# Half of an attention stage's transposes moved from TensorE to VectorE blocks and a DRAM round trip

## The chip, the cores and the metric

The kernel runs on one core of one Trainium2 chip, in one launch. The metric is the device time of that core in microseconds. A core has four engines that matter here: TensorE (PE in the profile, with PEld for its weight loads), VectorE (DVE), ScalarE (ACT) and GpSimd (POOL). Most transfers are issued from SyncE's queue (SP), some from POOL's. All engines run at the same time, and each takes its own instructions strictly in order.

## The reference

The reference is one layer of a diffusion backbone in float32, with 1024 latent tokens, 256 context tokens and 1024 channels: a gated feed-forward block (2816 wide), a mixer, a second feed-forward block and a final norm. The mixer holds a short gated convolution branch and an attention branch, merged by gates and one output projection. Only the attention is touched by the change:

```python
def gqa_attend(q, k, v):
    s = jnp.einsum('btkgd,blkd->bkgtl', q, k, preferred_element_type=jnp.float32) * (HEAD_DIM ** -0.5)
    p = jax.nn.softmax(s, axis=-1).astype(v.dtype)
    return jnp.einsum('bkgtl,blkd->btkgd', p, v)
```

There are 8 query heads of 128 channels that share 2 key and value heads. The 1024 latent queries look at 256 context keys and 1024 latent keys in one softmax.

## The kernel before

Every large product is made of three TensorE passes over a rounded high part and a remainder (`mm3`): high x high, high x low, low x high. So each operand is split by two instructions: ACT rounds it to the high part, and DVE (or POOL) subtracts that to get the low part (`split`).

The kernel goes through the first feed-forward block, the projections into the mixer, attention with the convolution branch mixed in, the merge and output projection, the second feed-forward block and the final norm. Large tiles (4 KB a partition) come from one ring of 38 buffers, `atile`; smaller ones from `ttile`, weights from `wpool`, and TensorE's results from 8 banks of PSUM in three groups (`ps_s` five, `ps_t` two, `ps_o` one).

Attention is cut into 16 units (`class Unit`), one for each query head and each half of the queries (512 queries, `C0` or `C1`). A unit does the following:

- `begin` splits its queries into parts.
- `scores(qt)`, four times, for 128 queries each: products with the 256 context keys and twice 512 latent keys, DVE maxima over them, and ACT exponentials that are written to `pc` (context keys) and to one `pl` tile for each `qt` (latent keys), with the sums of their rows.
- `turn(kt)`, ten times, for 128 keys each (`kt` 0 and 1 are context keys): the exponentials lie with queries on the partitions, but the product with the values needs keys there. So TensorE transposes four 128 x 128 blocks, one for each `qt`, into one PSUM bank of `ps_t`, and `split` makes the two parts `pts` from it.
- `values(kt)`: three 512-wide matmuls that add this block's share to the output.
- `inverse` takes the reciprocals of the sums and spreads them over the partitions by two small transfers on POOL's queue (`rinvd`, `rrow`); `output` copies the result from PSUM with ACT, and POOL multiplies it by these rows.

The generator `seconds` runs the turns and values of all units one after another, with values three turns behind the turns (`AHEAD`). The loop `for n_unit, u in enumerate(units[1:], 1)` puts the pieces together: while the scores of unit n are made, ten steps of `seconds` run, those of unit n - 1, in groups of 3, 2, 3 and 2, each behind one block of scores. Between them stand pieces of `fillers`, the convolution products, about ten a unit, until they run out some four units before the end. From unit 13 on, `split_output` splits finished heads on POOL. Behind the loop come the turns and values of the last unit, and `merge`.

The kernel is written as one program in this order. A planner then fixes the order of each engine's instructions by a simulated time of each, close to the program's order, and allots buffers. The semaphores follow from what reads and writes which tile.

## Time and profile before

| | us |
|---|---|
| median of 3 runs | 2631.33 |
| lowest and highest run | 2630.29, 2632.03 |
| span of the profiled execution | 2631.1 |
| TensorE busy in it | 2609.9 |
| VectorE busy | 1997.4 |
| ScalarE busy | 1183.5 |
| GpSimd busy | 545.8 |
| attention stage, about | 1434 to 1822 |

The profile is that of one execution. Its span runs from the first to the last instruction. An engine's busy time is the time in which at least one of its instructions runs; consecutive matmuls overlap, so the distance from start to start tells more than a duration does. A group's row has the instruction, what it writes and from what, its shape, how many there are, their busy time in us and the mean of one in ns, and then how long the engine was idle before them and for whom it waited. In this kernel all instructions carry line 90, a helper, so groups are told apart by the names of their tiles.

### The profile page before, as it was taken

What the parts mean: (1) busy time and instruction counts of PE and PEld (TensorE: products, weight loads), DVE (VectorE), ACT (ScalarE), POOL (GpSimd) and SP (SyncE); (2) the same over time, 40 slices, a digit from 0 to 9 for tenths busy, and PEclk for the clock granted to TensorE, in tenths of its full rate; (3) what the DMA queues carried; (4) which work ended last, traced back from release to release, by engine and by line L of the source; (5) the groups of instructions that cost most, each with busy time, mean ns of one, the idle gap of its engine ahead of it and who ended that gap; (6) DMA issues with size and microseconds to landing.
All of it is one profiled execution on the core that took longest, in us unless ns stands there. A gap on an engine that the chain in (4) does not pass through costs nothing.

```text
span 2631.1 us, 35379 instructions
## 1 busy us (share of the span) xinstructions
PE 2609.9 (99%) x12665; PEld 2176.1 (83%) x12665; DVE 1997.4 (76%) x3360; ACT 1183.5 (45%) x2343; POOL 545.8 (21%) x425
## 2 busy tenths in 40 slices
PE   8999999999999999999999999999999999999998
PEld 5888899888888888888888888888888888888888
DVE  5888976877897879977788576676457886667996
ACT  6533454333454642333355566574237333334553
POOL 0133201221010034333022112132000442321100
PEclk9999999999999999999999999999999999999999
DMA  8665465345973365542522322113425653227831
GB/s 324 205 210 182 149 215 173 106 131 185 327 184 117 124 205 160 163 134 89 200 77 85 86 87 65 33 37 118 158 85 176 201 167 96 90 80 286 191 84 65
DMA packets 372905, 384.69 MB, mean 146 GB/s; under 512 B 19686, under 2 KB 256376, under 8 KB 372728
## 3 DMA queue, kind: packets, MB, share of 16 engines
q1 hardware_dynamic: 363288, 363.52, 42.1%
q0 software_dynamic: 9440, 18.91, 4.3%
q8 instruction: 99, 1.62, 0.2%
q14 instruction: 78, 0.64, 0.1%
HBM read 310.45 MB, written 71.86 MB: 145 GB/s over the span
## 4 chain that ended last, share of the span: by engine, by line
PE 94%; DVE 3%; DMA 1%; ACT 1%; issue 1%; SPq 0%; DVEq 0%; ACTq 0%
PE ps L90 81%; PE pt L90 8%; PE po L90 6%; DMA rawm<-in_w_mod_dram 1%; DVE xb L90 0%; DVE wl L90 0%; DVE macc L90 0%; DVE m L90 0%; DVE y L90 0%; DVE pts L90 0%; DMA xtok<-in_x_dram 0%; DVE x L90 0%; DVE r L90 0%; SPq L90 0%; DVE rs_t L90 0%
## 5 line engine op out<-in xcount | busy, mean ns | idle before, releaser
L90 PE MATMUL ps<-r,wl 128*128 128x512 f32 x5196 | 1198.3, 390 | 3.6 <-ACT r L90 1.3
L90 PEld LDWEIGHTS ps<-r,wl 128*128 128x128 f32 x5196 | 972.4, 188 | 207.7 <-ACT r L90 1.6
L90 ACT CAST wl<-sum 128x512 fp32r<-128x512 f32 x218 | 134.1, 622 | 294.4 <-PE ps L90 227.1
L90 ACT CAST wl<-raw 128x512 fp32r<-128x512 f32 x287 | 178.2, 622 | 193.1 <-PE ps L90 147.9
L90 DVE TENSOR_TENSOR wl<-raw,wl 128x512 fp32r<-128x512 f32 x287 | 210.2, 736 | 61.0 <-ACT wl L90 59.3
L90 DVE TENSOR_TENSOR wl<-sum,wl 128x512 fp32r<-128x512 f32 x218 | 196.9, 904 | 33.5 <-ACT wl L90 32.3
L90 POOL TENSOR_TENSOR sum<-raw 128x512 f32<-128x512 f32 x55 | 76.4, 1389 | 680.6 <-DMA raw<-in_ffn_w_in_dram 345.3
L90 DVE SCALAR_TENSOR_TENSOR macc<-rawm,silu_c,macc 128x512 f32<-128x512 f32 x178 | 145.4, 835 | 17.1 <-DMA rawm<-in_w_mod_dram 16.6
L90 DVE TENSOR_TENSOR u<-u,ps 128x512 f32<-128x512 f32 x186 | 126.5, 680 | 32.2 <-PE ps L90 32.1
L90 ACT CAST rh<-hid 128x512 fp32r<-128x512 f32 x132 | 82.2, 623 | 139.4 <-PE ps L90 112.3
L90 POOL TENSOR_TENSOR sum<-raw,sum 128x512 f32<-128x512 f32 x55 | 76.7, 1395 | 287.0 <-DVE wl L90 284.0
L90 DVE TENSOR_TENSOR pts<-pt,pts 128x512 fp32r<-128x512 f32 x160 | 107.3, 686 | 36.2 <-ACT pts L90 34.6
L90 DVE TENSOR_REDUCE m<-ps 128x1 f32<-128x256 f32 (+1 forms) x192 | 111.0, 597 | 29.4 <-PE ps L90 28.5
L90 ACT CAST pts<-pt 128x512 fp32r<-128x512 f32 x160 | 92.2, 597 | 85.5 <-PE pt L90 84.4
L90 PE MATMUL ps<-rh,wl 128*128 128x512 f32 x360 | 122.8, 390 | 0.0
L90 PE MATMUL ps<-wh,r 128*128 128x512 f32 x384 | 120.7, 392 | 0.0
L90 DVE TENSOR_TENSOR rl<-hid,rh 128x512 fp32r<-128x512 f32 x132 | 91.0, 693 | 29.9 <-ACT rh L90 19.4
L90 ACT CAST wh<-raw 128x512 fp32r<-128x512 f32 (+1 forms) x85 | 68.2, 803 | 95.5 <-PE ps L90 74.9
L90 PE MATMUL ps<-kl,qs 128*128 128x512 f32 x384 | 104.0, 394 | 0.1
L90 PE MATMUL ps<-rh,wh 128*128 128x512 f32 x300 | 102.8, 389 | 0.0
L90 PE MATMUL ps<-y,wc 128*128 128x512 f32 x384 | 95.3, 391 | 0.2 <-DVE g L90 0.2
L90 POOL TENSOR_TENSOR sum<-sum,raw 128x512 f32<-128x512 f32 x55 | 87.8, 1597 | 5.7 <-PE ps L90 3.9
(325 smaller groups left out, 5102.3 us busy)
## 6 DMA issues: line engine op xcount, KB each, us to landing
raw<-in_ffn_w_in_dram SPq DMA_DIRECT2D x131, 512.0 KB
raw<-in_ffn_w_out_dram SPq DMA_DIRECT2D x72, 512.0 KB
raw<-in_w_in_dram SPq DMA_DIRECT2D x64, 512.0 KB
rawm<-in_w_mod_dram SPq DMA_DIRECT2D x104, 256.0 KB
hid<-hd SPq DMA_DIRECT2D x40, 512.0 KB
ucd<-uc SPq DMA_DIRECT2D x33, 512.0 KB
rawm<-in_w_mod_dram SPq DMA_DIRECT2D x32, 512.0 KB
ws<-in_ffn_w_out_dram POOLq DMA_DIRECT2D x26, 512.0 KB, 6.4
```

The source lines that it names most:

```text
L90: inst = getattr(self.engine, name)(*args, **kw)
```

## The change

The queries of each unit are now treated in two halves. For its last 256 queries (`qt` 2 and 3), and for the context keys of all its queries, nothing changes but the tiles: TensorE transposes them. For the latent keys of the first 256 queries (`qt` 0 and 1):

- ACT writes the exponentials to a tile `pb` of 2048 columns, ordered by key block of 32, then `qt`, then key.
- `place` is a generator that is called between the steps. Two DVE instructions transpose `pb` in place, 1024 columns each, block by block of 32 x 32. Then four transfers on SP, one for each 32 partitions, write the blocks to a DRAM tile `turned` in pieces of 64 floats, and a fifth reads them back as `placed`, with the 128 keys of a key block on the partitions and 256 queries beside each other for each of eight key blocks.
- `turn(kt)` for latent keys transposes two blocks instead of four, and the split is done in two halves of 256 columns: ACT and POOL for `placed`, ACT and DVE for the PSUM bank.
- The first 256 queries of an output come in the order of blocks, so `output` copies them with a rearranged pattern, in an instruction of its own; the context keys' transposes write PSUM in the same order.

The buffers are divided: the ring `atile` has 28 instead of 38, and the space of the other ten is a second pool, `btile`. Ahead of the attention loop that pool is closed and opened again as five buffers of twice the size (`share("Q", Q_BUFS)`), for `pb`, `pl` and `placed`; behind it, as ten again. Many tiles of the other stages are assigned to the one or the other.

```diff
-A_BUFS = 38
+A_BUFS, B_BUFS, Q_BUFS = 28, 10, 5
...
         def begin(self):
             self.qs = [ttile("qs", dt=F32R) for _ in range(2)]
             split(q_of(self.hd, self.ch), *self.qs)
-            self.pc = atile("pc", (P, 4, CT))
-            self.pl = []
-            self.rsum = small("rsum", 4)
+            self.pc, self.pb, self.pl = atile("pc", (P, 4, CT)), btile("pb", (P, 2048)), btile("pl", (P, 2, SLOT))
+            self.done, self.rsum = 0, small("rsum", 4)
...
+            blocks = self.pb[:].rearrange("p (j b q c) -> p j q b c", j=2, q=2, c=32)
             for j in range(2):
                 ps = ps_s()
                 kh, kl = (t[:, g] for t in k_lat[j])
                 mm3(ps, [(qh, ql, kh, kl)])
                 dve.reduce_max(out=m3[:, j + 1 : j + 2], in_=ps, axis=AX.X)
-                parts.append((pl[:, j * 512 : (j + 1) * 512], ps))
+                if qt < 2:
+                    parts.append((blocks[:, j, qt], ps.rearrange("p (b c) -> p b c", c=32)))
+                else:
+                    parts.append((self.pl[:, qt - 2, j * 512 : (j + 1) * 512], ps))
...
+        def place(self):
+
+            for half in range(2):
+                part = self.pb[:, half * 1024 : (half + 1) * 1024]
+                dve.transpose(out=part, in_=part)
+                yield
+            turned = dram.tile([32, 32, 4, 64], F32, name=uniq("turned"))
+            for i in range(4):
+                sp.dma_start(
+                    out=turned[:, :, i].rearrange("b r f -> r b f"),
+                    in_=self.pb[i * 32 : (i + 1) * 32].rearrange("r (b f) -> r b f", b=32),
+                )
+            yield
+            self.placed = btile("placed", (P, KD, 256))
+            sp.dma_start(out=self.placed[:], in_=turned.rearrange("(k j) r i f -> (j r) k (i f)", j=4))
+
         def turn(self, kt):
 
-            pt = ps_t()
-            for qt in range(4):
-                src = self.pc[:, qt, kt * P : (kt + 1) * P] if kt < 2 else self.pl[qt][:, (kt - 2) * P : (kt - 1) * P]
-                transpose(pt[:, qt * P : (qt + 1) * P], src)
             pts = wpool.tile([P, 2, 512], F32R, tag="wh", name=uniq("pts"), bufs=W_BUFS)
-            split(pt, pts[:, 0], pts[:, 1])
+            if kt < 2:
+                pt = ps_t()
+                first = pt[:, :256].rearrange("p (i q c) -> p q i c", i=4, q=2)
+                for qt in range(4):
+                    out = first[:, qt] if qt < 2 else pt[:, qt * P : (qt + 1) * P]
+                    transpose(out, self.pc[:, qt, kt * P : (kt + 1) * P])
+                split(pt, pts[:, 0], pts[:, 1])
+            else:
+                pt = ps_t(256)
+                for qt in range(2):
+                    transpose(pt[:, qt * P : (qt + 1) * P], self.pl[:, qt, (kt - 2) * P : (kt - 1) * P])
+                split(self.placed[:, kt - 2], pts[:, 0, :256], pts[:, 1, :256], pool)
+                split(pt, pts[:, 0, 256:], pts[:, 1, 256:])
             return pts
...
         def output(self):
             of = q_of(self.hd, self.ch)
-            act.copy(out=of, in_=self.po)
+            v = lambda t, by: t[:, :256].rearrange(by, i=4, q=2)
+            act.copy(out=v(of, "p (q i c) -> p q i c"), in_=v(self.po, "p (i q c) -> p q i c"))
+            act.copy(out=of[:, 256:], in_=self.po[:, 256:])
             pool.tensor_mul(out=of, in0=of, in1=self.rows)
...
     for qt in range(4):
         u.scores(qt)
+        if qt == 2:
+            place = u.place()
+            run(place, 2)
+        if qt == 3:
+            run(place)
         if qt < 3:
             run(conv_out(C0, 2 + qt))
             conv_weights(4 + qt)
...
         for n in (3, 2, 3, 2):
-            u.scores(len(u.pl))
+            u.scores(u.done)
+            if u.done == 3:
+                place = u.place()
             for _ in range(n):
+                if u.done > 2:
+                    run(place, 1)
                 run(rest, 1)
-                if len(u.pl) < 4:
+                if u.done < 4:
                     run(fill, 1)
```

More of the change, by code (lines that the diff above doesn't have):

```diff
@@ L105, in tile_dit_layer, with share @@
     dram = ctx.enter_context(tc.tile_pool(name="dram", bufs=1, space=DRAM))
+    shared = {}
+    def share(tag, bufs):
+        if shared:
+            shared.pop("guard").__exit__(None, None, None)
+        guard = tc.tile_pool(name=uniq("share"), bufs=bufs, reuse_waits="tile")
+        shared.update(guard=guard, pool=guard.__enter__(), tag=tag)
     n_tiles = [0]
@@ L423, in tile_dit_layer, with __init__ @@
     class Context:
-        def __init__(self, name, dt=F32):
-            self.t = [atile(name, (P, 4, CT), dt) for _ in range(2)]
+        def __init__(self, name, dt=F32, get=btile):
+            self.t = [get(name, (P, 4, CT), dt) for _ in range(2)]
         def __call__(self, k, ch=CC):
@@ L475, in fetch_rows @@
     def fetch_rows(w, js):
-        ts = {j: atile("raw") for j in js}
+        ts = {j: btile("raw") for j in js}
         for j, t in ts.items():
@@ L735, in start_by_half @@
         def start_by_half(self):
-            uc = [atile("uc", (P, 2, 512)) for _ in range(2)]
+            uc = [btile("uc", (P, 2, 512)) for _ in range(2)]
             def second(j, t):
@@ L1402, in v_tile @@
         return v_hi[(kt - 2) // 4][:, (kt - 2) % 4], v_lo[(kt - 2) // 4][:, (kt - 2) % 4]
-    rope_t = [atile("rope", (P, KD, HD)) for _ in range(2)]
+    rope_t = [btile("rope", (P, KD, HD)) for _ in range(2)]
     for i in range(2):
         sp.dma_start(out=rope_t[i][:], in_=rope[i])
-    hg = atile("hg", (P, 2, HD))
+    hg = btile("hg", (P, 2, HD))
     pg = ps_t(2 * P)
@@ L1694, in merge @@
         yield
+    share("Q", Q_BUFS)
     units = [Unit(hd, ch) for hd in range(NQ) for ch in (C0, C1)]
@@ L1744, in tile_dit_layer @@
     split_output(NQ - 1, C1, late=True)
+    share("B", B_BUFS)
     for j in range(KD):
@@ L1752, in tile_dit_layer @@
     fast = Winograd(xs, None, modl, 6, column_pairs(ffn2_w_in[0], ffn_offsets), ahead=AH3)
+    fast.shared_forms = [(i, k) for i in (4, 7, 6) for k in range(4)][:B_BUFS]
     first = fast.norm0()
@@ L1861, in tile_dit_layer @@
     run(finals[2])
+    shared["guard"].__exit__(None, None, None)
 _INS = [
```

55 lines of the change are left out of this document (29 added, 26 removed).

## The prediction

> **What bounds the kernel now.** I read the page's totals and its chain of waits first.
>
> ```profile
> span 2631.1 us, 35379 instructions
> PE 2609.9 (99%) x12665; PEld 2176.1 (83%) x12665; DVE 1997.4 (76%) x3360; ACT 1183.5 (45%) x2343; POOL 545.8 (21%) x425
> PE 94%; DVE 3%; DMA 1%; ACT 1%; issue 1%; SPq 0%; DVEq 0%; ACTq 0%
> PE ps L90 81%; PE pt L90 8%; PE po L90 6%; DMA rawm<-in_w_mod_dram 1%; DVE xb L90 0%; DVE wl L90 0%; DVE macc L90 0%; DVE m L90 0%; DVE y L90 0%; DVE pts L90 0%; DMA xtok<-in_x_dram 0%; DVE x L90 0%; DVE r L90 0%; SPq L90 0%; DVE rs_t L90 0%
> ```
>
> TensorE is busy 99% of the span and carries 94% of the chain, so any work taken off it shortens the run, as long as nothing new makes it wait. All idle time of TensorE together is 2631.1 - 2609.9 = 21.2 us.
>
> The attention stage comes next, in the view of busy time by stretches. The first stretch is four units while convolution products ("fill") are mixed in, the second four units at the end of the loop, after these have run out (the stretches run from one unit's `rinvd` transfer to that of the fourth after it). Columns: length, then PE, PEld, DVE, ACT, POOL, clock, DMA share, GB/s.
>
> ```profile
> 1550.16:1645.82 95.66, 95.49 (x517) 80.28 (x516) 59.67 (x130) 57.92 (x146) 20.16 (x16) 1.00 0.20 59
> 1718.99:1792.34 73.35, 72.47 (x415) 60.31 (x413) 55.00 (x125) 54.05 (x143) 32.20 (x38) 1.00 0.19 48
> ```
>
> A unit takes 95.66/4 = 23.9 us with fill and 73.35/4 = 18.3 us without. Without fill DVE has 55.00/4 = 13.75 us of work in each, ACT 13.5, POOL 8.05. TensorE sets the pace at full clock in both, but the second kind has far less room on the other engines.
>
> **What the change takes away.** The price of one transpose is read from the order of time on TensorE (start, duration):
>
> ```profile
> 1603.51 1.03 PE L90 MATMUL pt<-ident,pc 128*128 128x128 f32 x8
> 1604.30 0.48 PE L90 MATMUL ps<-pts,vh 128*128 128x512 f32 x1
> 1614.23 0.60 PE L90 MATMUL pt<-ident,pl 128*128 128x128 f32 x4
> 1614.58 0.49 PE L90 MATMUL po<-pts,vh 128*128 128x512 f32 x1
> 1614.91 0.39 PE L90 MATMUL po<-pts,vl 128*128 128x512 f32 x1
> 1615.14 0.39 PE L90 MATMUL po<-pts,vh 128*128 128x512 f32 x1
> 1615.37 0.60 PE L90 MATMUL pt<-ident,pl 128*128 128x128 f32 x4
> 1618.91 0.52 PE L90 MATMUL ps<-kc,qs 128*128 128x256 f32 x3
> 1619.26 0.87 PE L90 MATMUL ps<-kl,qs 128*128 128x512 f32 x3
> L90 PE MATMUL pt<-ident,pl 128*128 128x128 f32 x512 | 76.6, 273 | 1.5 <-DVE pts L90 1.4
> ```
>
> The durations overlap, so starts count. Eight transposes push the next matmul back by 0.79 us, four by 0.35: 0.44 for four more, 0.11 each. The check: one step (four transposes, three 512-wide matmuls at 0.23, as from 1614.91 to 1615.14) lasts 1615.37 - 1614.23 = 1.14 = 4 x 0.11 + 0.70. Of the 512 transposes of `pl` half go (two of four, eight key blocks, 16 units): 256 x 0.11 = **28.2 us**, 1.76 us a unit. The pace that the other engines must hold becomes 18.3 - 1.76 = 16.6 us without fill.
>
> **What it adds beside TensorE.** Rows of the attention stage (count, busy us, mean ns):
>
> ```profile
> L90 ACT CAST pts<-pt 128x512 fp32r<-128x512 f32 x160 | 92.2, 597 | 85.5 <-PE pt L90 84.4
> L90 ACT ACTIVATE pl<-ps,nm 128x512 f32<-128x512 f32 x128 | 87.3, 693 | 0.0
> L90 ACT ACTIVATE pc<-ps,nm 128x256 f32<-128x256 f32 x64 | 30.9, 483 | 41.8 <-DVE nm L90 41.7
> L90 DVE TENSOR_TENSOR pts<-pt,pts 128x512 fp32r<-128x512 f32 x160 | 107.3, 686 | 36.2 <-ACT pts L90 34.6
> L90 DVE TENSOR_REDUCE m<-ps 128x1 f32<-128x512 f32 x126 | 84.4, 686 | 13.9 <-PE ps L90 13.1
> L90 DVE TENSOR_REDUCE m<-ps 128x1 f32<-128x256 f32 x63 | 26.4, 420 | 15.5 <-PE ps L90 15.4
> L90 DVE TENSOR_TENSOR wc<-raw,wc 128x1024 fp32r<-128x1024 f32 x3 | 3.7, 1219 | 0.5 <-ACT wc L90 0.5
> L90 POOL TENSOR_TENSOR wc<-raw,wc 128x1024 fp32r<-128x1024 f32 x9 | 21.6, 2400 | 10.3 <-ACT wc L90 10.2
> L90 POOL TENSOR_TENSOR ol<-q,oh 128x512 fp32r<-128x512 f32 x14 | 17.9, 1286 | 0.0
> ```
>
> DVE: the subtraction of eight key blocks shrinks from 512 to 256 columns; by the two maxima 256 columns save 686 - 420 = 266 ns, so -2.13 us a unit. Two block transposes of 1024 columns are added. No row shows one. The nearest is DVE's subtraction of the same width, 1.22 us; half and twice that are my ends (0.61, 2.44). I take 1.22: DVE has 13.75 - 2.13 + 2.44 = 14.1 of 16.6 us and costs nothing; at the upper end 16.5, level with the unit, so little more.
>
> By the Trainium skill, "VectorE: DVE Perf Modes", section "The three transpose paths", a 128 x 128 block-wise transpose of 2-byte data takes VectorE 311 ns. Eight of them for 1024 columns would be an estimated 2.49 us, and DVE would be as long as the unit without fill.
>
> ACT: one 512-wide cast becomes two of 256; by the exponentials 256 columns are worth 693 - 483 = 210 ns, so a 256-wide cast is about 387 and eight key blocks cost 8 x (2 x 387 - 597) = 1.4 us more, the split output copy 0.2. ACT has 13.5 + 1.6 = 15.1 of 16.6 us: covered, with 1.5 us to spare. The exponentials now write pieces of 32 columns. No such row; the columns are as many, so I take 0; were the four affected ones doubled (+2.8 us a unit), ACT would exceed the unit by 1.3.
>
> POOL: eight subtractions of 256 columns, 1286 - (2400 - 1286)/2 = 729 ns each, 5.8 us a unit. POOL has 8.05 + 5.8 = 13.9 of 16.6.
>
> **The path through DRAM.** This is what can be late. Each unit writes 1 MB as four transfers of 1024 pieces of 256 B and reads it back as 1024 pieces of 1 KB; the read waits on SP for all four writes, and ACT's cast for key block 2 of the next unit waits for the read. Piece prices come from two stretches, one of nearly only 512 B pieces (60 us), one of 2 KB pieces (150 us); the fixed part from the first and the last transfers.
>
> ```profile
> q1 hardware_dynamic: 11458, 5.79, 32.8%
> raw<-in_w_out_dram SPq DMA_DIRECT2D x9, 512.0 KB
> q1 hardware_dynamic: 11253, 21.52, 40.4%
> 1.54 0.29 SPq L90 DMA_DIRECT2D vraw<-in_norm_g_dram  x1
> 3.16 0.27 PE L90 MATMUL pt<-ident,vraw 24*128 24x24 f32 x1 [3.16 <-DMA vraw<-in_norm_g_dram]
> 2626.30 0.99 SPq L90 DMA_DIRECT2D out_dram<-ot  x2
> ```
>
> 0.328 x 60 x 16 / 11458 = 27.5 ns for 512 B on one of 16 engines; 0.404 x 150 x 16 / 11253 = 86 ns, about 94 for the 2 KB pieces without the small completion records. The line through 27.5 and 94 gives 16 ns at 256 B and 49 at 1 KB. No row has 256 B writes; I bound them by 16 ns (the line) and 27.5 (no cheaper than 512 B) and take the middle, 22: 256 pieces per engine are 5.6 us. A read lands 3.16 - 1.54 = 1.6 us after issue; a write at most 2631.1 - 2627.3 = 3.8 after issue, less the last transfer's own 1.5 (128 pieces of twice 94 ns over 16) = 2.3. The whole way: four issues at about 0.35 = 1.4, writes 5.6, landing 2.3, issue 0.3, read 64 x 0.049 = 3.1, landing 1.6: **14.3 us** (12.8 at 16 ns, 15.7 at 27.5).
>
> The cover: score blocks take 0.35 + 2 x 0.70 = 1.74 us (three 256-wide, six 512-wide matmuls), a step now 0.92 (1.14 for the two context blocks), a fill piece 0.69. From the transfers' place in the third group of steps to key block 2 of the next unit lie four steps, two score blocks, two context steps and fill: 11.3 us with fill. ACT then stands, with the exponentials queued behind it; TensorE goes on until the fifth turn (key block 4) lacks one of two PSUM banks: 0.92 + 0.69 + 1.74 + 0.92 + 0.69 = 5.0 later. Cover 16.2 us with fill, 12.1 without, 8.6 at the end, where the last unit has no scores behind it. The first unit has its two DVE transposes ahead of a convolution product (5.5 us) and is covered.
>
> So units with fill lose nothing; three handovers without fill lose 14.3 - 12.1 = 2.2 each, the end 5.7: 12.3 us. SP stands some 8 us at the read; behind it are loads and stores that convolution uses a unit later, 23.9 us: nothing. The ring of 38 buffers divided 28 to 10 I cost at nothing: loads run far enough ahead that TensorE idles 21.2 us in the whole span; what it costs without that cover is a rival below.
>
> **The sum:** -28.2 + 12.3 = -15.9 on the profiled span of 2631.1, which is 0.2 from the median 2631.33: **2615 us**.
>
> **The rivals.** *POOL takes over (2629).* POOL's queue holds each unit's two small transfers, the second of which waits for the first to land:
>
> ```profile
> 1718.99 0.80 POOL L90 DMA_DIRECT2D rinvd<-rinv  x1 [11.70 <-DVE rinv L90]
> 1727.59 0.56 POOL L90 DMA_DIRECT2D rrow<-rinvd  x1 [7.81 <-DMA rinvd<-rinv]
> ```
>
> The new subtractions queue behind that 7.8 us stand. If nothing is put into it, a unit costs POOL 13.9 + 7.8 = 21.7 us against 16.6: four units without fill lose 20.4 in place of 6.6, with the end 26.1, and -2.1 is left. For it: the stand is in every unit. Against: a unit with fill holds 5.0 + 5.8 + 7.8 = 18.6 in 22, and some subtractions come ahead of the wait.
>
> *The placing is late in every unit (slower, 2722 at its worst).* At the point where the way exceeds 16.2 us, above 29.5 ns a piece, the eleven units with fill lose too. It eats the gain at 16.8 us, 32 ns a piece. If a 256 B write costs two 512 B accesses, 55 ns, the way is 22.8 us and the loss 11 x 6.6 + 3 x 10.7 + 14.2 = 119 us: +91. For it: 32 ns is only a little over the 512 B price. Against: bytes alone make it 16. The Trainium skill, "DMA: Bandwidth & Descriptors", section "Specifications", gives 512 B as the least for line rate and says smaller ones are read, modified and written; no run here shows it yet.
>
> *The change takes back elsewhere what it gives (2637).* If the divided buffer ring makes loads late in the other stages and doubles TensorE's idle time, +21.2 turns -15.9 into +5.3. Against: TensorE's 21.2 us of idle time hardly leave room for a stage that is already short of buffers. That the removed transposes weren't on the path can't be at 99% busy.
>
> **How the numbers follow.** Forecast 0.57, POOL 0.13, late placing 0.20, buffers 0.10. The forecast's own range is 2603 (nothing lost) to 2624 (27.5 ns a piece gives 2621, and slower ACT pieces). 8 in 10 needs the near part of the late placing, up to 37 ns a piece: 2603 to 2652. About 0.2%, 5 us, is what a measurement of this kernel can tell. Faster: 0.57 and 0.03 of POOL's 0.13, 0.60; the same: 0.07 of POOL and 0.03 of the buffers, 0.10; slower: the rest, 0.30.
>
> **What would show it.** In the new profile: 256 `pl` transposes instead of 512, steps of 0.92 us; DVE transposes near 1.2 us; the read landing some 14 us after the first write's issue; waits of ACT for `placed` only after the convolution has run out; POOL's `pts` near 0.73 us. ACT waits for `placed` in units with fill, TensorE waiting for POOL, or more idle time outside attention would make the prediction wrong.

## The result, and the profile after

The changed kernel takes 2695.53 us against 2631.68 for the one before in the same comparison: a ratio of 1.0238, 95% interval 1.0224 to 1.0252. One of its four runs took 4363 us at a granted clock of 0.56 instead of 0.99; the ratio leaves it out, and without it the median is 2695.13. The kernel is slower by some 63 us; 2615 had been forecast. The profiled execution has a span of 2694.2 us, 63.1 more than before, and it is the one that the rest explains.

The page of the kernel after, its totals:

```profile
span 2694.2 us, 35524 instructions
PE 2617.8 (97%) x12409; PEld 2157.7 (80%) x12409; DVE 2005.3 (74%) x3392; ACT 1197.9 (44%) x2487; POOL 635.6 (24%) x553
```

The 256 transposes are gone (12665 instructions on TensorE before, 12409 now), yet TensorE is busy for 7.9 us longer.

Where the time lies is read from the view of busy time by stretches, with borders at the first transpose of a `pc` tile and the end of the last one of a `pl` tile. First before, then after (length; PE, PEld, DVE, ACT, POOL; clock, DMA share, GB/s):

```profile
0.00:1443.80 1443.80, 1433.98 (x6918) 1193.95 (x6919) 1172.26 (x1965) 633.97 (x1234) 311.69 (x237) 1.00 0.53 170
1443.80:1808.70 364.90, 361.55 (x1980) 301.83 (x1979) 244.16 (x525) 230.94 (x582) 88.17 (x84) 1.00 0.23 62
1808.70:2631.10 822.40, 814.37 (x3771) 680.33 (x3769) 580.99 (x872) 318.58 (x529) 145.97 (x104) 1.00 0.46 141
```

```profile
0.00:1449.40 1449.40, 1437.48 (x6919) 1193.85 (x6920) 1176.69 (x1966) 633.51 (x1234) 311.29 (x237) 1.00 0.53 170
1449.40:1865.00 415.60, 359.50 (x1726) 283.77 (x1723) 248.13 (x556) 246.41 (x724) 176.32 (x211) 0.95 0.53 133
1865.00:2694.20 829.20, 820.80 (x3771) 680.12 (x3768) 580.47 (x872) 318.03 (x531) 147.99 (x106) 1.00 0.45 140
```

So 63.1 = 5.6 ahead of attention + 50.7 in it + 6.8 behind it. In attention TensorE stands for 415.60 - 359.50 = 56.1 us, before for 3.35. Its busy time fell by 2.1 only, although 28 us of transposes are gone, and the clock fell from 1.00 to 0.95. Behind attention TensorE stands no longer than before (8.4 us against 8.0) and the instructions are the same, and still it takes 6.4 us more of busy time.

The prices of the operations, in the groups of the attention stage of the kernel after (count, busy us, mean ns):

```profile
L90 POOL TENSOR_TENSOR pts<-placed,pts 128x256 fp32r<-128x256 f32 x128 | 92.2, 737 | 62.0 <-ACT pts L90 55.9 <-DVE pts L90 5.9
L90 ACT CAST pts<-placed 128x256 fp32r<-128x256 f32 x128 | 53.5, 422 | 59.0 <-POOL pts L90 15.3 <-DMA placed<-turned 15.2 <-PE po L90 12.6
L90 PE MATMUL pt<-ident,pl 128*128 128x128 f32 x256 | 51.0, 284 | 10.4 <-DVE pts L90 8.8 <-DVE nm L90 1.2
L90 ACT CAST pts<-pt 128x256 fp32r<-128x256 f32 x128 | 48.6, 384 | 40.4 <-PE pt L90 40.3
L90 DVE STREAM_TRANSPOSE pb<-pb 128x1024 f32<-128x1024 f32 x32 | 39.1, 1237 | 15.3 <-ACT pb L90 12.4 <-POOL pts L90 1.4 <-DMA g<-gcd 0.8
```

And one undisturbed step on TensorE, in order of time:

```profile
1640.03 0.48 PE L90 MATMUL po<-pts,vh 128*128 128x512 f32 x1
1640.34 0.40 PE L90 MATMUL po<-pts,vl 128*128 128x512 f32 x1
...
1640.95 0.48 PE L90 MATMUL po<-pts,vh 128*128 128x512 f32 x1
```

From 1640.03 to 1640.95 are 0.92 us: the step is as short as forecast, and the operations of these rows are within a tenth of the forecast prices (ScalarE's 422 ns against 387 is the farthest). What went wrong lies mostly between the operations.

Who waits for whom in attention (columns: us in total, times, the longest), first TensorE, then GpSimd, then ScalarE, all of the kernel after:

```profile
PE po L90 <- POOL pts L90: 17.8, 5, 6.0
PE ps L90 <- POOL pts L90: 13.3, 4, 4.8
PE pt L90 <- DVE pts L90: 9.3, 14, 2.3
PE ps L90 <- ACT pts L90: 6.7, 1, 6.7
...
POOL rrow L90 <- DMA rinvd<-rinv: 81.5, 11, 10.2
...
ACT pts L90 <- DMA placed<-turned: 15.2, 3, 10.3
```

TensorE's matmuls wait for parts `pts` from three engines, most for GpSimd's. GpSimd stands for the small transfer of the row sums, and the placed subtractions are queued behind it. (In the kernel before it stood there for 96.2 us, but no parts `pts` were queued behind it.) ScalarE stands for `placed`. That makes three suspects, beside the divided ring.

The worst single stall, in order of time:

```profile
1640.09 5.30 SPq L90 DMA_DIRECT2D turned<-pb  x4
...
1647.61 0.78 POOL L90 DMA_DIRECT2D rinvd<-rinv  x1 [2.26 <-DVE pts L90]
1648.28 0.38 SPq L90 DMA_DIRECT2D placed<-turned  x1
...
1663.49 0.40 ACT L90 CAST pts<-placed 128x256 fp32r<-128x256 f32 x1 [10.29 <-DMA placed<-turned]
...
1665.08 0.79 PE L90 MATMUL ps<-pts,vh 128*128 128x512 f32 x1 [6.66 <-ACT pts L90]
...
1666.01 0.78 PE L90 MATMUL ps<-pts,vh 128*128 128x512 f32 x1
1666.58 0.63 PE L90 MATMUL ps<-pts,vl 128*128 128x512 f32 x1
```

The read takes 15.2 us from issue to use, with the 4-byte pieces of `rinvd` on the way beside it. After TensorE's 6.66 us the next matmul of the same pair starts 0.57 us later (1666.01 to 1666.58) where 0.31 is normal (1640.03 to 1640.34). The stretch view says the same of the clock, 0.50 in the last column but two, from the first matmul behind the stand on:

```profile
1665.08:1671.34 6.26, 6.26 (x17) 4.99 (x18) 4.86 (x10) 4.25 (x12) 5.07 (x5) 0.50 0.14 31
```

The Trainium skill, "TensorE: Matmul & The Clock Gate", section "Part 1: The HAM clock gate", says that about 3.4 us of idling put TensorE to half its clock until it has been busy again for as long. The trace agrees in kind: the clock fell to 0.50 in the middle of the stand of 6.66 us. The times differ: it fell some 2.7 us after the last matmul had ended (1658.4 to 1661.1), and it came back only 6.3 us after matmuls had begun again (1665.08 to 1671.3).

### The profile page after: what moved, and what is told of

Same layout as the page of the kernel before. It is cut to its first block, busy times and chain, and to the rows that moved or that the text cites. A ratio compares the mean times of both kernels' runs of the same rounds, so it can differ in the third digit from the quotient of the medians.

```text
span 2694.2 us, 35524 instructions
## 1 busy us (share of the span) xinstructions
PE 2617.8 (97%) x12409; PEld 2157.7 (80%) x12409; DVE 2005.3 (74%) x3392; ACT 1197.9 (44%) x2487; POOL 635.6 (24%) x553
## 5 line engine op out<-in xcount | busy, mean ns | idle before, releaser
L90 DVE TENSOR_TENSOR wl<-raw,wl 128x512 fp32r<-128x512 f32 x287 | 209.6, 733 | 66.7 <-ACT wl L90 65.1
L90 PE MATMUL ps<-kl,qs 128*128 128x512 f32 x384 | 109.7, 413 | 4.3 <-ACT pc L90 4.3
L90 POOL TENSOR_TENSOR pts<-placed,pts 128x256 fp32r<-128x256 f32 x128 | 92.2, 737 | 62.0 <-ACT pts L90 55.9
L90 DVE TENSOR_TENSOR pts<-pt,pts 128x256 fp32r<-128x256 f32 (+1 forms) x160 | 74.0, 470 | 33.5 <-ACT pts L90 31.1
L90 POOL DMA_DIRECT2D ws<-in_ffn_w_out_dram x30 | 35.4, 1245 | 263.5 <-PE ps L90 121.2
```

Source lines behind the costliest of these rows:

```text
L90: inst = getattr(self.engine, name)(*args, **kw)
```

## The experiments

All results in one table. The attention stage has the borders used above; "stands" is its length less TensorE's busy time in it, both from the stretch view.

| kernel | median us | ratio to before, 95% | attention us | TensorE stands | clock |
|---|---|---|---|---|---|
| after | 2695.5 | 1.0238 [1.0224, 1.0252] | 415.6 | 56.1 | 0.95 |
| e3_buffers | 2654.0 | 1.0082 [1.0067, 1.0097] | 371.8 | 8.4 | 0.99 |
| e6_buffers_pad | 2645.8 | 1.0052 [1.0037, 1.0067] | 371.8 | 8.1 | 0.99 |
| e7_before_shift | 2635.2 | 1.0011 [1.0002, 1.0021] | 364.8 | 3.3 | 1.00 |
| e1_rows_sp | 2690.4 | 1.0225 [1.0208, 1.0242] | 403.0 | 48.7 | 0.95 |
| e2_sub_dve | 2684.6 | 1.0195 [1.0180, 1.0211] | 402.6 | 47.7 | 0.95 |
| e5_no_path | 2679.2 | 1.0179 [1.0164, 1.0195] | 396.0 | 40.8 | 0.96 |
| e4_rows_sp_sub_dve | 2719.4 | 1.0337 [1.0320, 1.0355] | 436.5 | 71.0 | 0.93 |
| e8_rows_sp_sub_dve_no_path | 2693.1 | 1.0234 [1.0219, 1.0249] | 416.9 | 54.3 | 0.94 |
| e10_sub_dve_no_path | 2678.4 | 1.0170 [1.0154, 1.0186] | 393.5 | 40.7 | 0.97 |
| e11_rrow_late | 2698.3 | 1.0241 [1.0224, 1.0258] | 425.8 | 61.5 | 0.94 |
| e12_early | 2693.8 | 1.0227 [1.0210, 1.0245] | 406.3 | 50.0 | 0.95 |
| e13_late_early_pad | 2687.2 | 1.0201 [1.0177, 1.0224] | 417.8 | 55.0 | 0.94 |
| e14_pool_order | 2714.9 | 1.0315 [1.0299, 1.0330] | 430.6 | 67.7 | 0.93 |
| e15_pool_order_early_pad | 2702.4 | 1.0262 [1.0245, 1.0279] | 430.8 | 65.1 | 0.92 |
| e16_lag | 2675.5 | 1.0156 [1.0141, 1.0171] | 394.6 | 39.5 | 0.95 |
| e17_lag_pool_pad | 2668.6 | 1.0133 [1.0116, 1.0150] | 394.9 | 41.7 | 0.96 |
| e18_halves | 2687.1 | 1.0209 [1.0192, 1.0226] | 405.8 | 26.8 | 0.99 |
| e19_traffic | 2716.4 | 1.0320 [1.0304, 1.0335] | 441.6 | 54.0 | 0.95 |

**The divided ring alone.** `e3_buffers` keeps the ring of 28, the second pool and every tile's assignment outside attention, and does attention as before: all transposes on TensorE, no placing.

```diff
-            self.pc, self.pb, self.pl = atile("pc", (P, 4, CT)), btile("pb", (P, 2048)), btile("pl", (P, 2, SLOT))
+            self.pc, self.pl = atile("pc", (P, 4, CT)), [btile("pl", (P, 2, SLOT)) for _ in range(2)]
...
-        if qt == 2:
-            place = u.place()
```

> The attention as before (TensorE transposes all four blocks, no DVE transposes, no path through DRAM), with the changed kernel's division of the buffers: the ring of 28 and the second pool, and in attention two double-size pl tiles a unit from it. Buffer theory: most of the 64 us are here, 2660 to 2700. POOL and DRAM theories: the division costs at most the 5 us by which attention starts later in the changed kernel, 2630 to 2640.

It takes 2654.0 us, 21.9 more than before in its comparison, between the ranges of the theories. Its stretches (the first row ends where attention begins):

```profile
0.00:1449.40 1449.40, 1436.15 (x6919) 1192.33 (x6920) 1177.22 (x1965) 632.24 (x1234) 310.57 (x237) 1.00 0.53 170
1449.40:1821.20 371.80, 363.41 (x1981) 303.08 (x1980) 247.72 (x525) 231.54 (x582) 87.88 (x84) 0.99 0.25 58
1821.20:2650.30 829.10, 820.79 (x3771) 680.22 (x3769) 580.41 (x872) 317.71 (x529) 146.74 (x104) 1.00 0.45 140
```

So the division brings 5.6 us ahead, 6.9 in attention and 6.7 behind, without any of the change's work. The 6.7 are no waits: before, 8.0 us of the last stretch are not busy, here 8.3. The matmuls themselves are longer. I followed the distance from start to start of 512-wide matmuls to the next one of the same group, by the tile that streams through (which tile lies in which pool follows from the program, not from the trace; over all of this group behind attention the means are 229.3 in e3 and 226.8 in e6):

```
behind attention, ps<-r,wl         matmuls  mean ns  over 232 ns
kernel e3, r tile in the second pool   660    232.8   328
kernel e3, r tile in the ring         1183    228.7    43
kernel e6, r tile in the second pool   660    226.7     1
```

The ring's tiles start at 3328 + 4096 n bytes, a multiple of 256. The second pool starts at 188032, 128 bytes past one. Two runs ask whether that is it: `e6_buffers_pad` is e3 with a small unused tile ahead of the second pool, so that it starts at 188160; `e7_before_shift` puts one of 128 bytes ahead of the ring of the kernel before.

```diff
+    spool.tile([P, 8], F32, tag="pad", name="pad")
```

```diff
+    const.tile([P, 32], F32, name="pad")
     apool = ctx.enter_context(tc.tile_pool(name="apool", bufs=A_BUFS))
```

> The kernel of before with the divided ring alone (no turning by VectorE, no transfers), and an unused tile of 32 bytes x 4 buffers ahead of the second pool, so that its tiles start at a multiple of 256 bytes (188160) instead of 128 bytes past one (188032). Without the pad this kernel takes 2654.0 us; its matmuls with an operand in the second pool start 229 to 237 ns apart, those with both in the first pool 226.7. Theory 'start address': the odd 128 bytes cost it; with the pad all of them are at 226.7, the stage behind attention goes from 829.1 to 822 to 824 us and the total to 2634 to 2642. Rival 'place': the upper end of the memory is slower to read, whatever the start; 2652 to 2656, stage behind 829. Rival 'order': the ring's shortness delays loads; 2652 to 2656, too.

> The kernel before with an unused tile of 128 bytes ahead of its ring, so that the ring, the weights and the working tiles all start 128 bytes past a multiple of 256 (3456 instead of 3328). Nothing else is changed. Theory 'start address': every matmul of 512 columns that streams from these tiles goes from 226.7 to 229 to 237 ns; with some 7800 such matmuls at 5 ns on the average the total goes to 2660 to 2690. Rival 'place': 2630 to 2634. Theory 'two operands that start differently' (a first-pool and a second-pool tile in one matmul): 2630 to 2634, too, since all are shifted together.

e6 takes 2645.8 us, 8.2 less than e3 (forecast 2634 to 2642), and the stage behind attention is back at 822.6, as forecast. The group's rows behind attention, of e3 and then of e6, show it in their means:

```profile
L90 PE MATMUL ps<-r,wl 128*128 128x512 f32 x1848 | 425.1, 392 | 1.0 <-ACT uc L90 1.0
```

```profile
L90 PE MATMUL ps<-r,wl 128*128 128x512 f32 x1848 | 420.3, 389 | 1.0 <-ACT uc L90 1.0
```

e7 moves everything by 128 bytes and its stage behind attention stays at 822.4 us, its total 2.8 above before. So the start alone costs next to nothing here; tiles with different starts in one chain of matmuls do. Whether it is the stream against the weights or against the stream before it wasn't tried. The other 14 us stay with the division: e6 still has 1449.40 us ahead and 371.80 in attention. Whether the shorter ring makes them or the tiles' new places in the two pools wasn't separated.

**One late item at a time.** Three edits of the kernel after: the row sums' two transfers on SP's queue instead of GpSimd's; the placed subtraction on VectorE; the placed tile read from another array that was written long ago (the values of the first 256 queries are left out by that, no work is).

```diff
-            pool.dma_start(out=row.rearrange("(j p) -> p j", p=P), in_=rinv[:])
+            sp.dma_start(out=row.rearrange("(j p) -> p j", p=P), in_=rinv[:])
...
-            pool.dma_start(out=self.rows, in_=row.partition_broadcast(P))
+            sp.dma_start(out=self.rows, in_=row.partition_broadcast(P))
```

> The changed kernel, but with the two small transfers of each unit (rinvd, rrow) on SP's queue instead of POOL's. POOL theory (TensorE waits because POOL's new subtractions stand behind the 7 to 10 us in which rrow waits for rinvd): POOL waits for no transfer any more, TensorE's idle time in the attention stage falls from 56 us to under 25, the waits of PE and PEld for POOL's pts (together 65 us) nearly go, and the time falls by 30 to 60 us, to 2635 to 2665. DRAM theory (the placed tile arrives late): POOL is only the messenger, at least 2685 remains. Buffer theory (the divided ring): unchanged, 2690 to 2700.

```diff
-                split(self.placed[:, kt - 2], pts[:, 0, :256], pts[:, 1, :256], pool)
+                split(self.placed[:, kt - 2], pts[:, 0, :256], pts[:, 1, :256])
```

> The changed kernel, but the low part of the placed half is subtracted by DVE instead of POOL (128 subtractions of 256 columns, about 0.42 us each, 3.4 us a unit more on DVE); the small transfers stay on POOL. POOL theory: no pts comes from POOL, so its waits harm nobody but the output product; 2630 to 2660, with DVE at about 18 of 22 us. DRAM theory: at least 2685. Buffer theory: 2690 to 2700.

```diff
-            sp.dma_start(out=self.placed[:], in_=turned.rearrange("(k j) r i f -> (j r) k (i f)", j=4))
+            sp.dma_start(out=self.placed[:], in_=xd[:, :, :256].rearrange("k p n -> p k n"))
```

> The changed kernel, but the tile placed is read from another DRAM tensor of the same shape of pieces that is long written (the residual), so that the read waits for no write; all writes, transposes and subtractions are still done, and the values of the first 256 queries are left out of the computation (they are not the attention's). DRAM theory: the stalls go, the time falls by 40 us or more, to 2655 or less. POOL theory: only the 15 us in which ACT waited for the transfer can go, 2675 to 2695. Buffer theory: 2690 to 2700.

They take 2690.4, 2684.6 and 2679.2 us: 5, 11 and 16 less than the kernel after. No theory holds in all three: e1 is where the buffer theory put it (and above the DRAM theory's bound), e2 is a little below that bound, and e5 is where the POOL theory put it, with the 16 us of the late transfer. In e1 TensorE's waits for GpSimd are gone and others stand in their place (the longest times in attention):

```profile
PE ps L90 <- ACT pc L90: 13.4, 7, 8.7
PE pt L90 <- DVE pts L90: 13.3, 20, 2.1
```

e1 is no clean test of GpSimd's queue. The stand for the row sums has only moved: SP now has it, 136.9 us in attention, and ScalarE stands 32.1 us for the placed tile where it stood 15.2.

**Two and three at a time.** e4 has the first two edits, e8 all three, e10 the second and the third.

> The kernel after with the placed subtraction on VectorE and both transfers of the row sums on SP's queue: GpSimd takes no part in the placed exponentials. Theory 'the stalls replace one another' (each late item alone gave back 4 to 16 us): the two gains add up to no more than 20 us, 2672 to 2682, and TensorE waits for VectorE's pts and for pc. Theory 'GpSimd' (its queue of both transfer and subtraction is the one cause): 2645 to 2660, the attention stage at 375 to 385 us instead of 415.6.

> As e4_rows_sp_sub_dve, and the placed tile is read from another array in DRAM that has been there for long, so no read waits for the four writes (the values of the first 256 queries of each unit are left out; every instruction and byte is the same). All three late items are gone. Theory 'late items': nothing is left but the work, 2632 to 2645 (before, less 28 for the transposes, plus 22 for the divided ring, plus some 10). Rival 'load': VectorE's and ScalarE's added work itself does not fit beside TensorE in order, and the stage stays at 390 us or more: 2660 to 2675.

> As e8_rows_sp_sub_dve_no_path, but both transfers of the row sums stay on GpSimd's queue as in the kernel after (the placed subtraction on VectorE; the placed tile read from an array that has been there for long, so the values of the first 256 queries are left out). Theory 'SP stands': in e8 SP stood 131 us for the 4-byte pieces of the row sums to land, and everything SP loads or places came late; with them off SP and nothing else late, the attention stage falls to 370 to 385 us and the total to 2645 to 2660. Rival 'load': the added work on VectorE and ScalarE does not fit in order; stage 395 or more, total 2675 to 2690.

e4 takes 2719.4 us, more than either edit alone and more than the kernel after; e4 and e8 are both slower than all their theories had it. A cause stands in SP's waits, here of e8, where the read waits for no write:

```profile
SPq L90 <- DMA rinvd<-rinv: 131.4, 16, 9.0
```

SP stands 131 us for the row sums, as GpSimd did, and now loads and writes are queued behind it: ScalarE waits 31.1 us for the placed tile in e8, though nothing has to be written first. e10 differs from e8 only in the queue of these two transfers and takes 14.7 us less; ScalarE's wait for the tile is 9.2 us there. But its attention stage is still 393.5 us, where the theory of the late items had 370 to 385; its total of 2678.4 is in the range of the rival, the added work in order. Three quarters of TensorE's 40.7 us of standing are now a wait for VectorE, which has taken over GpSimd's subtractions:

```profile
PE pt L90 <- DVE pts L90: 30.4, 28, 4.9
```

**The order in GpSimd's queue.** e11 asks for `rrow` three steps later, e12 begins the placing one block of queries earlier, e13 has both and the pad. In e11 the planner set the transfer back to right behind `rinvd`, so e14 and e15 hold `rinvd`, `rrow` and the placed subtractions to the program's order (e15 with the early placing and the pad).

```diff
             if kt == 4:
                 u.inverse()
+            if kt == 7:
+                u.spread()
```

```diff
-            if u.done == 3:
+            if u.done == 2:
                 place = u.place()
...
-                if u.done > 2:
+                if u.done > 1:
                     run(place, 1)
```

```diff
+                tc.keep_in_program_order(pool.tensor_sub(out=pts[:, 1, :256], in0=self.placed[:, kt - 2], in1=hi.bitcast(F32)))
...
+            tc.keep_in_program_order(pool.dma_start(out=self.rows, in_=self.row.partition_broadcast(P)))
```

> The kernel after, with the spreading of the row sums (rrow) issued three steps later, after the values of block 7 instead of block 4, so that GpSimd no longer stands behind the landing of rinvd (81.5 us of standing in after) while placed subtractions wait in its queue. Theory 'GpSimd's standing starves TensorE of pts': the 46 us in which TensorE waits for GpSimd's pts go, but the placed read's lateness (25 us) and VectorE's share stay: 2665 to 2680, POOL's wait for rinvd under 30 us. Rival 'the stalls replace one another in full': 2685 to 2697.

> The kernel after, with the turning and placing of each unit begun one block of queries earlier (behind the scores of queries 128 to 255, which is as soon as its exponentials exist, instead of behind those of 256 to 383). Nothing else changed. Theory 'placed too late': ScalarE's 25 us of standing for the placed tile (in windows where it was the last) go, and GpSimd's remains: 2675 to 2688. Rival 'the transposes now stand in VectorE's queue in front of maxima': TensorE waits more for pc, 2695 to 2710.

> The kernel after with three edits: rrow issued after block 7, placing begun one block of queries earlier, and the pad that lets the second pool start at a multiple of 256 bytes. If the two late items were all that stalled attention, its stage comes to 360 to 375 us (before 364.9, less 28.2 for the transposes, plus 6.9 for the shorter ring, plus 15 to 30 that stay), the stage behind to 822.5, and the total to 2635 to 2650; if VectorE's and ScalarE's order is a cause of its own, the stage stays at 390 or more and the total at 2660 to 2675.

> As e11_rrow_late, where the planner put the spreading of the row sums back right behind rinvd, in front of the next unit's placed subtractions (in e11 GpSimd stood 95.5 us for rinvd); here rinvd, rrow and the placed subtractions are held to the program's order on GpSimd, so that the unit's remaining subtractions stand between the two. Theory 'GpSimd's order starves TensorE of pts': its standing for rinvd falls to under 30 us, TensorE's 46 us of waiting for GpSimd's pts falls to under 10, the attention stage from 415.6 to 375 to 395 us, the total to 2655 to 2680. Rival 'the stalls replace one another': the standing moves to VectorE's pts and the maxima; 2685 to 2700.

> e14_pool_order with placing begun one block of queries earlier and the second pool at a multiple of 256 bytes. The pad gives 6.5 us behind attention whatever the theory. If GpSimd's order and the late placing are what is left of the loss, the attention stage comes to 355 to 375 us and the total to 2630 to 2650; if ScalarE's work in order (18.6 us in a unit without filling work, against TensorE's 16.5) sets the pace, the stage stays at 380 to 400 and the total at 2655 to 2675.

e11 and e12 changed nothing that can be told from the kernel after, and e13 gained little more than the pad. In e14 the waits of TensorE's matmuls for GpSimd shrank from 17.8 + 13.3 us to 8.1 + 2.4, as the theory said, and yet the kernel became 19 us slower. GpSimd's own stand for the row sums fell to 67.5 us only, where the theory had under 30. One row of ScalarE's grew much:

```profile
ACT pts L90 <- DMA placed<-turned: 48.5, 9, 8.4
```

It stands 48.5 us for the placed tile, against 15.2 in the kernel after. What GpSimd no longer held up may have come to a stand one wait later; no run shows that the one made the other. The placing one block earlier (e15) left that at 48.0. e13, e14 and e15 are all slower than either theory had them.

**More cover.** In e16 a unit's turns and values lag five of their ten steps further behind its scores. So that the buffers suffice, the read goes into the unit's own `pb`, which is free by then. e17 adds the order of GpSimd's queue and the pad.

```diff
-            self.placed = btile("placed", (P, KD, 256))
-            sp.dma_start(out=self.placed[:], in_=turned.rearrange("(k j) r i f -> (j r) k (i f)", j=4))
+            self.placed = self.pb[:].rearrange("p (k n) -> p k n", k=KD)
+            sp.dma_start(out=self.placed, in_=turned.rearrange("(k j) r i f -> (j r) k (i f)", j=4))
...
-                run(rest, 1)
+                if n_unit > 1 or u.done > 2:
+                    run(rest, 1)
```

> The kernel after with two edits: the placed tile is read into the unit's own pb (free once its blocks are written), so that a unit holds two tiles of the second pool instead of three, and the turning and the values of every unit lag five of their ten steps further behind its scores. The path from the exponentials to ScalarE's first cast of the placed tile took 15 us (1739.9 to 1754.9) to 20; the lag adds some 10 us of other work in front of that cast. Theory 'the DRAM path is longer than its cover, and what stands then moves from engine to engine': ScalarE no longer stands for the placed tile (under 5 us), the attention stage comes to 370 to 390 us and the total to 2650 to 2670, GpSimd's share being left. Rival 'ScalarE's and VectorE's work in order sets the pace': stage 395 or more, total over 2675.

> e16_lag with GpSimd's queue held to the program's order and rrow issued behind the unit's last placed subtraction (as in e14, where TensorE's waiting for GpSimd fell from 46 to 18 us and ScalarE's standing for the placed tile rose to 48), and the second pool at a multiple of 256 bytes (6.5 us). If path and queue order together are the loss in the attention stage, it comes to 345 to 365 us (before 364.9, less 28.2, plus 6.9 for the ring) and the total to 2620 to 2640; if the work in order sets the pace, the stage is at 385 or more and the total at 2660 or more.

They take 2675.5 and 2668.6 us, the best of the kernels that place. ScalarE's waits of e17 hold no more than this for the placed tile:

```profile
ACT pts L90 <- DMA pb<-turned: 0.3, 1, 0.3
```

So the path through DRAM is fully covered, and the attention stage is still 394.9 us. That is what the rival of the work in order had for e17 (385 or more); for e16 it had 395 or more, against 394.6. TensorE's waits in e17 are small and many:

```profile
PE pt L90 <- DVE pts L90: 13.6, 14, 2.4
PE po L90 <- POOL pts L90: 8.2, 5, 3.9
PE ps L90 <- ACT pc L90: 6.4, 6, 2.5
```

But the row sums are not out of the way in it. GpSimd still stands for both of their transfers, for the first before it issues the second, and for the second before it multiplies an output by the rows; in sum that is longer than the 81.5 us of the kernel after, and placed subtractions are queued behind both:

```profile
POOL rrow L90 <- DMA rinvd<-rinv: 53.9, 9, 9.7
POOL q L90 <- DMA rrow<-rinvd: 33.0, 8, 4.7
```

In e16 it stands 97.8 us for `rinvd`, and TensorE waits 19.2 us for its parts; in e17 13.0.

**The added work without the placed tile.** To find the rest, two kernels start from e3: e18 only casts and subtracts the latent blocks in two halves; e19 only adds block transposes, writes and read of a tile that nobody uses.

```diff
-            split(pt, pts[:, 0], pts[:, 1])
+            if kt < 2:
+                split(pt, pts[:, 0], pts[:, 1])
+            else:
+                split(pt[:, :256], pts[:, 0, :256], pts[:, 1, :256])
+                split(pt[:, 256:], pts[:, 0, 256:], pts[:, 1, 256:])
```

```diff
+            sp.dma_start(out=self.pb[:].rearrange("p (k n) -> p k n", k=KD), in_=turned.rearrange("(k j) r i f -> (j r) k (i f)", j=4))
```

> The divided ring alone (as e3_buffers: all transposes on TensorE, no block transposes, no transfers, 2654.0 us, attention stage 371.8), but for the latent blocks the two halves of 256 queries are cast by ScalarE and subtracted by VectorE in instructions of their own, as the change does it for one of them: 8 casts and 8 subtractions more per unit. Theory 'ScalarE's and VectorE's work in order sets the pace': in units without filling work ScalarE comes from 16.8 to 18.5 us against TensorE's 18.3, and the stage grows to 385 to 400 us, total 2667 to 2685. Rival 'halving costs little': stage 371 to 378, total 2653 to 2660.

> The divided ring alone (as e3_buffers, 2654.0 us), and beside it, per unit, the two block transposes on VectorE, the four writes and the read through DRAM of a tile whose content nobody uses, issued where the change issues them. Nothing waits for the read but the next unit's transposes. Theory 'contention': 2.5 us per unit of VectorE and the second MB each way on the DMA engines delay maxima and loads: stage 385 to 400 us, total 2667 to 2685. Rival 'only what waits for the placed tile costs': stage 372 to 378, total 2654 to 2661.

Both are dear, 33 and 62 us above e3 and above the ranges of both theories, and neither is a clean answer. In e18 ScalarE waits for VectorE between the halves, which the kernel after doesn't do (its row above, 40.4 us of idling, has TensorE alone):

```profile
L90 ACT CAST pts<-pt 128x256 fp32r<-128x256 f32 x256 | 91.5, 380 | 101.9 <-PE pt L90 63.4 <-DVE pts L90 35.8 <-PE ps L90 0.5
```

In e19 the one tile makes each unit's block transposes wait for the read of the unit before, in front of VectorE's other work:

```profile
DVE pb L90 <- DMA pb<-turned: 57.7, 13, 9.5
```

The new waits (35.8 and 57.7 us) are of the size by which the attention stages grew over e3 (34.0 and 69.8); that the one makes the other is argued, not shown. What neither shows is how the halved casts or the traffic would do without these waits.

## Why the prediction was wrong

**Right.** The transposes: 256 fewer, and the step of 0.92 us stands in the trace; by that step -28.2 us is what they would have given. VectorE's block transpose takes 1.237 us (1.22 taken), GpSimd's subtraction 737 ns (729), ScalarE's 256-wide casts 384 and 422 (387). The 311 ns that the Trainium skill, "VectorE: DVE Perf Modes", section "The three transpose paths", has for 128 columns of 2-byte data did not carry over to this float32 tile: 1.237 us for 1024 columns are 155 ns for 128.

**The ring "I cost at nothing".** This step failed first: 21.9 us by e3. Some 8 of them (2654.0 - 2645.8; 6.5 by the profiles) come from start addresses, of which the prediction had no notion; the other 14 from the division itself. The reason given, that loads run far enough ahead, says nothing of the addresses, and TensorE's idle time in the whole span did rise, from 21.2 to 30.0 us in e3. The rival at a chance of 0.10 had the right size, 21.2 us, but by luck: it had that idle time doubling, and the rest came as slower matmuls.

**"Units with fill lose nothing".** This step failed most. In the stretch view from the first `rinvd` to the twelfth, eleven units with fill, and from there to the last, the four without (the prediction shows their 73.35 us before), this is first the kernel before, then the kernel after:

```profile
1457.73:1718.99 261.26, 259.02 (x1409) 216.34 (x1409) 172.09 (x372) 163.82 (x412) 49.50 (x42) 1.00 0.23 62
```

```profile
1463.26:1751.27 288.01, 255.09 (x1237) 203.59 (x1237) 174.69 (x395) 174.40 (x511) 111.01 (x129) 0.95 0.54 134
1751.27:1844.64 93.37, 74.72 (x354) 58.07 (x353) 57.27 (x134) 58.94 (x180) 53.77 (x67) 0.91 0.44 112
```

By the forecast the eleven units come to 261.3 - 11 x 1.76 = 241.9 us; they take 288.0, 46 more. The four without fill come to 73.4 - 7.0 + 6.6 = 72.9 and take 93.4, 20 more. So the larger part of the 79 us between forecast and profiled span lies where nothing was to be lost, though each unit without fill misses by slightly more (5.1 us against 4.2), and the 2.2 us for each of its handovers was too little. (By e3 some 7 us of the two parts are the division's.) Two of the units with fill, 23.9 us before, look like this in the kernel after:

```profile
1578.89:1600.24 21.35, 21.22 (x109) 17.31 (x108) 14.91 (x35) 15.04 (x45) 10.65 (x12) 1.00 0.46 110
1647.61:1679.39 31.78, 25.12 (x111) 20.29 (x110) 13.36 (x31) 14.96 (x44) 10.62 (x12) 0.84 0.61 111
```

The first shows a gain of the forecast's size, the second loses 8 us. No engine is full in either: ScalarE's 15 us and GpSimd's 10.6 are the same in both. The prediction had compared busy times with the unit's length and called what fits "covered". But each engine takes its work in a fixed order. In POOL's rival it did see the subtractions queue behind the row sums' landing, and then cleared the units with fill by a sum (18.6 in 22). In the trace the subtractions do stand there, in a unit with fill:

```profile
1600.24 0.79 POOL L90 DMA_DIRECT2D rinvd<-rinv  x1 [2.70 <-DVE pts L90]
1610.64 0.56 POOL L90 DMA_DIRECT2D rrow<-rinvd  x1 [9.62 <-DMA rinvd<-rinv]
1611.22 0.74 POOL L90 TENSOR_TENSOR pts<-placed,pts 128x256 fp32r<-128x256 f32 x1
```

**The path of 14.3 us.** Its length was near in a quiet unit and its parts were not. There it ran as follows:

```profile
1741.83 3.92 SPq L90 DMA_DIRECT2D turned<-pb  x4
...
1748.87 0.38 SPq L90 DMA_DIRECT2D placed<-turned  x1
...
1754.90 0.71 ACT L90 CAST pts<-placed 128x256 fp32r<-128x256 f32 x2
```

From the first write's issue to the cast are 13.1 us; the four issues take 3.9 (1.4 forecast), and the rest is shorter than forecast. In the worst unit it is 23.4 (1640.09 to 1663.49). SP's stand at the reads, put at 8 us each, was 3.5 us at the longest (33.5 in attention). The cover's text counts four steps, but its sums (11.3 and 12.1) hold three, which is what the program has. The rival of late placing had such a path at 22.8 and a chance of 0.20, but the path is not the cause in the main: with no wait for the writes (e5) 16 us come back, with a longer cover (e16) 20, of 63 lost.

**A stall costs more than its length.** The prediction priced stalls at their own time. In attention the sum is 371.8 (e3) - 28.2 + 47.7 more standing + 24.3 of slower work = 415.6. The 24.3 is what remains of busy time: 359.50 - (363.41 - 28.2). The clock of 0.95 against e3's 0.99 is worth an estimated 0.04 x 359.5 = 14 of it; a part of the rest may be that the profile counts a matmul's modelled tail as busy when nothing follows. So each us of standing took about half a us more with it. The clock can't be all: e18, at 0.99, has 15.6 us more of busy time than e3 beside 18.4 more of standing.

**What stays open.** Taking away GpSimd's subtractions (e2), the wait for the writes (e5) or both (e10), and even full cover of the path (e16, e17), all end at 393 to 403 us of attention, where the division and the transposes alone would make 343.6. From 50 to 60 us remain, and their cause stays open. What the runs do show is that no single late item holds them, and that no run is free of all: in e10 TensorE waits for VectorE, which has more to do; in e16 and e17 GpSimd still stands for the row sums, ahead of placed subtractions. A lagged kernel with the row sums' transfers on a queue that nothing else needs wasn't tried, nor a longer distance from turns to values (`AHEAD`). So two explanations are left beside each other: the stands in GpSimd's queue, and ScalarE's and VectorE's added work in order, which e18 and e19 don't settle. None of the kernels with the placing reached the kernel before.

## What to carry to other kernels

Busy time that fits is no cover: for every engine that is given work, write down what stands ahead of it in its queue and what that waits for, and price TensorE's standing above its length (here about one and a half times). When several waits are nearly equally late, removing one shows the next. An edit that moves a wait to another queue, or work to another engine, does not remove it: look who stands now (SP in e1, e4 and e8, VectorE in e10). Moving tiles between pools is an edit of its own: test it alone, and let all pools whose tiles meet in one matmul chain start at the same offset from 256 bytes.

## What had not been expected of the hardware

- The 128 bytes: 512-wide matmuls with a streamed tile of the second pool followed each other at 232.8 ns on the mean instead of 226.7, until the pool was shifted by 128 bytes; shifting all tiles of the kernel before by 128 bytes left its stage behind attention at 822.4 us.
- The transfer of 512 row sums in pieces of 4 bytes takes 9.3 us from issue to landing (the median in the row below, of the kernel after's view of DMA issues; the prediction had seen one stand of 7.81), and SP stood up to 9.0 us for it in e8. Beside it the 1 MB read was used 15 us after its issue in the worst unit; in the quiet one, at 1748.87, 6 us after.

```profile
rinvd<-rinv POOLq DMA_DIRECT2D x16, 2.0 KB, 9.3
```

- In a stand of 6.66 us the granted clock fell to 0.50 after some 2.7 us, and stayed there for 6.3 us after matmuls had begun again.
